# The short convolution's three input projections as seven-multiplication block products

## The chip, the cores and the metric

The kernel runs on one core of one Trainium2 chip. The metric is the device time in microseconds (us) of the whole program, median of three runs. The core has TensorE (PE, matmuls; weight loads are shown as PEld), VectorE (DVE), ScalarE (ACT), GpSimd (POOL) and SyncE (SP, which here only issues DMAs; ScalarE's queue issues some too). All data is float32.

## The reference

A decoder trunk of two layers over 1024 tokens of width 1024. Each layer: a mixer, cross-attention into 256 memory tokens, a squared-ReLU MLP, each behind an RMSNorm and with a residual add. Layer 0's mixer is attention with pooling; layer 1's mixer, which the change is about, is a short gated convolution:

```
def odd_mixer(h, w_in, conv_w, w_out):
    proj = h @ w_in                                  # 1024 -> 3 * 1024
    b_gate = proj[..., :CONV_DIM]
    c_gate = proj[..., CONV_DIM:2 * CONV_DIM]
    z = c_gate * proj[..., 2 * CONV_DIM:]
    zp = jnp.pad(z, ((0, 0), (CONV_WIDTH - 1, 0), (0, 0)))
    y = zp[:, 0:S] * conv_w[0]
    for tap in range(1, CONV_WIDTH):                 # CONV_WIDTH = 3
        y = y + zp[:, tap:tap + S] * conv_w[tap]
    return (b_gate * y) @ w_out
```

## The kernel before, in words

Activations lie transposed: 8 tiles of 128 channels x 1024 tokens. Every float32 matmul operand is cut into a high part `hi` (a rounding copy on ScalarE) and a low part `lo` (what is left, a subtraction on VectorE) by `cut`. A product is then three matmuls, hi*hi, hi*lo and lo*hi, of 128 x 128 weights against 512 tokens.

There are two forms of product. `gemm` makes one tile of 128 output channels: 8 k tiles x 3 x 2 token halves = 48 matmuls (line 201). `split_gemm` makes a pair of output tiles as a 2x2 block product in seven multiplications instead of eight: 7 parts x 4 k pairs x 3 = 84 matmuls (line 277) where two calls of `gemm` have 96. It needs combinations of blocks on both sides. On the weight side `w_cut` makes them from a pair of weight tiles (lines 132 to 160) with four VectorE operations. On the operand's side the class `Split` holds four groups per pair of k tiles: group 0, 1 and 2 of 1024 columns and group 3 of 512, each cut in hi and lo; `combine` (line 257) makes groups 1 to 3 from the scaled raw halves with four VectorE operations. The seven parts accumulate in three PSUM banks, and after each part an `evac` copies or adds a bank to the result (`SPLIT` and `ADDS`; `TAIL` and `TAIL_ADDS` are another order of the same seven, with nine instead of seven additions, in which the first half of both tiles is done after the fifth part). With `first=True` the first four parts run their first three k pairs before the last one, so that the operand's last pair may come late. `hooks` give functions that are called ahead of part i.

The MLP up-projections and down-projections and the cross-attention's queries already use `split_gemm`. The convolution (`conv_mixer`, line 1152) uses `gemm` for its 24 output tiles: for each of 8 channel tiles the gate c, the value x and the gate b; VectorE multiplies each straight out of PSUM, and the norm's factor `rbc` (of the RMSNorm, which is computed beside the first products) is multiplied in there. Its operand is a plain `Act`: 8 pairs of hi and lo. It is made at the end of the first MLP (`mlp`, line 1018, called with the name "m0"): the down-projection m0b runs over four blocks of hidden units c and, for each, four pairs p of output tiles. In each of these 16 products the residual tiles `t` come from DRAM (`look` calls `h_load`) and the parts are added to them; for c < 3 they go back to DRAM (`keep`), and for c = 3 `done` makes the operand of them and adds their squares to the norm (`nn.add`). `A[c]`, the hidden operand, is a `Split` whose groups are fetched from DRAM.

After the projections `residual` (line 828) runs conv_out (named cvo in the profile), one `gemm` per output tile, over `Y`, the 8 tiles of gated results, cut by `Y.put`.

The tile framework's scheduler lays the instructions of each engine in a fixed order at compile time, by readiness and by program order (`tc.high_priority` moves the evacuations ahead). Each engine, SP's and ScalarE's DMA queues too, then works strictly in that order, and waits by semaphores. SBUF has 44 slots of 128 x 1024 (`NSLOT`) for all activations, 4 raw weight tiles (`WR`) and 2 cut ones of each kind; a new weight tile is fetched when a raw one is free (`w_load`, line 113), and cutting runs at most one step ahead of use (`w_next`).

Of the kernel before, what the change touches and what calls it, by code (L numbers as in the profile page):

```python
# [11 lines left out]
F32 = mybir.dt.float32  # L12
# [28 lines left out]
def hybrid_trunk(ctx: ExitStack, tc: tile.TileContext, xT, memT, vecs, lams, rel, onehot, negrow, invcnt,  # L41
# [39 lines left out]
    FLAT = (P, KT, P)  # L81
    order = [(FLAT, w_in[8])]
    for h in range(1, 4):
# [15 lines left out]
    tails = {len(order) - 1}  # L99
    raws, cuts = {}, []  # L100
# [727 lines left out]
    def residual(act, g_col, name, split=False):  # L828
# [3 lines left out]
        r = [None, None]  # L832
        for n in range(KT):
            t = ahead.pop(0)
# [21 lines left out]
            else:  # L856
                ps = gemm(act, f"{name}_{n}")
                nc.vector.tensor_add(t, t, ps)
# [159 lines left out]
    def mlp(l, X, nrm, g_next, name):  # L1018
# [75 lines left out]
        rest = {}  # L1094
        nx, nn = Act(), Norm(f"{name}b")
        fin = g_next is None
        for c in range(4):
            for p in range(KT // 2):
                t, ahead = ahead, []
                tail = fin and c == 3 and p == KT // 2 - 1  # L1100

# [5 lines left out]
                def squares_of(n, h):  # L1107
                    return lambda: nn.add(t[n][:, half(h)], h)
# [4 lines left out]

                todo = [rest, {1: [look]}]
                if p == 0:
# [3 lines left out]
                if c == 0 and p < 2:  # L1119
                    todo.append(late[p])  # L1120
                if tail:
                    todo.append({3: [squares_of(0, 0)], 5: [squares_of(1, 0)], 6: [squares_of(1, 1), lambda: nn.stage1((0,))]})
# [5 lines left out]

                def done(i, t=t, p=p):
                    def run():  # L1130
                        n = 2 * p + i
                        if fin:
                            hd[n] = t[i]
                        else:
                            operand(nx, n, t[i], g_next, f"{name}b")
                        nn.add(t[i])
                    return run

                if c < 3:
                    rest = {2: [keep]}  # L1140
                elif tail:
                    hd.update({2 * p + i: t[i] for i in range(2)})
                    squares_of(0, 1)()
                    rest = {}
                else:
                    rest = {1: [done(0)], 2: [done(1)], 4: [] if fin else [keep]}
        for fns in merged(rest).values():
# [4 lines left out]
    def conv_mixer(X, nrm, g_next, name):  # L1152
        hooks = with_norm(nrm)
        Y = Halves()
        for j in range(KT):
            nm = f"{name}{j}"
            psc = gemm(X, f"{nm}c", hooks.pop(0) if hooks else None)
            cg, z = slot(f"{nm}_cg"), slot(f"{nm}_z")
            if nrm.rbc is not None:
                nc.vector.tensor_mul(cg, psc, nrm.rbc)  # L1160
            psx = gemm(X, f"{nm}x", hooks.pop(0) if hooks else None)
            if j == 0:
                nc.vector.tensor_mul(cg, psc, nrm.rbc)
            nc.vector.tensor_mul(z, psx, nrm.rbc)
            nc.vector.tensor_mul(z, z, cg)
            y = slot(f"{nm}_y")
            nc.scalar.activation(y, z, AF.Copy, scale=col(C_CONV + 16 + j))
            nc.vector.scalar_tensor_tensor(y[:, 1:], z[:, : S - 1], col(C_CONV + 8 + j), y[:, 1:],
                                           op0=ALU.mult, op1=ALU.add)
            nc.vector.scalar_tensor_tensor(y[:, 2:], z[:, : S - 2], col(C_CONV + j), y[:, 2:],  # L1170
                                           op0=ALU.mult, op1=ALU.add)
            nc.vector.tensor_mul(y, y, nrm.rbc)
            psb_ = gemm(X, f"{nm}b")
            nc.vector.tensor_mul(y, y, psb_)
            Y.put(f"{nm}g", j, y)
        return residual(Y, g_next, f"{name}o", split=True)

# [30 lines left out]
def _layout(inp):  # L1208
# [38 lines left out]
    g["pool_w"] = a["pool_w"][0].transpose(1, 0, 2)  # L1247
    g["conv_in"] = tiles(a["conv_w_in"][0])
# [4 lines left out]
    halves = [0, 2, 4, 6, 1, 3, 5, 7]  # L1253
    g["wq"] = tiles(a["xattn_wq"])[..., halves, :]
    g["w1"] = tiles(a["mlp_w1"])[..., halves, :]
# [22 lines left out]
```

## Time and profile before

| | |
|---|---|
| median of three runs | 2549.22 us (2549.22, 2549.35, 2545.19) |
| the profiled execution | 2544.53 us; its span 2542.8 us |
| mean granted TensorE clock | 0.997 |
| PE, PEld, DVE, ACT busy | 98%, 81%, 69%, 42% of the span |
| TensorE instructions | 11522 matmuls (transposes among them) and as many weight loads |
| HBM | 249.91 MB read, 114.03 MB written |

The time holds a launch beside the span of 1.7 us in the profiled execution. A row of the profile's groups reads: line, engine, operation, output <- inputs by the program's names with shapes, count, busy us, mean ns of one, and idle time before it with what ended it. Names: m0a and m0b are the first MLP's up- and down-projection, cv0c, cv0x, cv0b to cv7b the 24 convolution products, cvo conv_out, c1q the next cross-attention's queries; `_x` and `_yz` are PSUM banks, `wr`, `wt`, `wh`, `wl` raw, combined, high and low weights. A matmul's own duration includes its passage through the array, so the distance between starts is what counts.

### The profile page before, as it was taken

The numbers are of one execution on the slowest core, as the hardware profiler recorded it, in microseconds if no ns is written. First come the engines' busy times: TensorE is split into PE (matmuls) and PEld (weight loads), VectorE is DVE, ScalarE is ACT, GpSimd is POOL, SyncE is SP. The second block draws the span as 40 slices with busy tenths as digits, with TensorE's granted clock in tenths as the row PEclk, the third lists the DMA queues.
The fourth block names the chain that finished last, engine by engine and source line by source line (L and its number), as shares of the span: only waits on it lengthen the run. The fifth ranks groups of instructions, "written<-read, shape, count | busy, mean of one in ns | idle before, by whom it ended". The sixth has DMA issues, their size and how long they took to land.

```text
span 2542.8 us, 29713 instructions
## 1 busy us (share of the span) xinstructions
PE 2498.8 (98%) x11522; PEld 2048.1 (81%) x11522; DVE 1763.8 (69%) x2339; ACT 1073.4 (42%) x1513; POOL 25.7 (1%) x24
## 2 busy tenths in 40 slices
PE   9999999999999999999999999999999999999997
PEld 6777778888878888788888888888887888778886
DVE  7777764766677777888784433576667777888876
ACT  5455664445443334443341111344544333434432
POOL 0000000000000000000000000000000000000001
PEclk9999999999999999999999999999999999999998
DMA  5111255221424346877641111422133444777752
GB/s 175 34 34 42 75 169 204 100 83 42 141 88 171 139 145 239 293 270 261 243 154 59 50 50 46 145 75 92 58 117 116 159 160 153 269 266 259 281 207 92
DMA packets 108429, 365.88 MB, mean 144 GB/s; under 512 B 12416, under 2 KB 14848, under 8 KB 108288
## 3 DMA queue, kind: packets, MB, share of 16 engines
q1 hardware_dynamic: 74880, 252.82, 29.5%
q10 hardware_dynamic: 33408, 111.16, 11.4%
q8 instruction: 91, 1.49, 0.2%
q14 instruction: 50, 0.41, 0.0%
HBM read 249.91 MB, written 114.03 MB: 143 GB/s over the span
## 4 chain that ended last, share of the span: by engine, by line
PE 89%; DVE 6%; ACT 2%; DMA 2%; issue 1%; POOL 0%; SPq 0%; ACTq 0%; DVEq 0%; POOLq 0%
PE m0a_x L277 7%; PE m1a_x L277 7%; PE m1b_x L277 7%; PE m0b_x L277 6%; PE m1a_yz L277 5%; PE m0a_yz L277 5%; PE m1b_yz L277 5%; PE m0b_yz L277 4%; PE cvo L201 3%; PE X L201 3%; PE c1o L201 3%; PE c0o L201 3%; PE kv_ps L742 3%; PE qkv L201 2%; PE c1q_x L277 2%; PE c0q_x L277 2%
## 5 line engine op out<-in xcount | busy, mean ns | idle before, releaser
L72 ACT ACTIVATE wh<-wr 128x1024 fp32r<-128x1024 f32 (+1 forms) x318 | 305.6, 961 | 777.7 <-PE m1b_yz L277 137.5
L73 DVE TENSOR_TENSOR wl<-wr,wh 128x1024 fp32r<-128x1024 f32 (+1 forms) x318 | 350.3, 1101 | 135.1 <-ACT wh L72 130.3
L72 ACT ACTIVATE wh<-wt 128x1024 fp32r<-128x1024 f32 x72 | 76.0, 1055 | 60.0 <-PE m0b_x L277 16.5
L73 DVE TENSOR_TENSOR wl<-wt,wh 128x1024 fp32r<-128x1024 f32 x72 | 87.8, 1219 | 0.9 <-ACT wh L72 0.9
L201 PE MATMUL X<-Y,wh 128*128 128x512 f32 x256 | 69.8, 389 | 0.0
L581 ACT ACTIVATE s_p<-s,s_negm 128x128 f32<-128x128 f32 (+7 forms) x64 | 47.3, 739 | 33.6 <-DVE s_negm L580 30.3
L201 PEld LDWEIGHTS X<-Y,wh 128*128 128x128 f32 x256 | 48.1, 188 | 10.0
L149 DVE TENSOR_TENSOR wt<-wr 128x512 f32<-128x512 f32 x71 | 48.8, 687 | 6.8 <-DMA wr<-in_w_dram 3.1
L150 DVE TENSOR_TENSOR wt<-wr,wt 128x512 f32<-128x512 f32 x71 | 48.9, 689 | 1.3
L152 DVE TENSOR_TENSOR wr<-wr,wr 128x512 f32<-128x512 f32 x71 | 48.7, 687 | 1.0
L153 DVE TENSOR_TENSOR wr<-wr,wt 128x512 f32<-128x512 f32 x71 | 48.6, 684 | 0.0
L1028 ACT ACTIVATE m0a_r<-m0a_r 128x1024 f32<-128x1024 f32 x32 | 33.9, 1061 | 32.0 <-DVE m0a_r L1027 31.9
L1028 ACT ACTIVATE m1a_r<-m1a_r 128x1024 f32<-128x1024 f32 x32 | 33.9, 1060 | 32.0 <-DVE m1a_r L1027 31.8
L580 DVE TENSOR_REDUCE s_negm<-s 128x1 f32<-128x128 f32 (+7 forms) x64 | 46.6, 750 | 0.2
L1042 DVE TENSOR_TENSOR m0a_r<-m0a_r,m0a_yz 128x512 f32<-128x512 f32 x32 | 21.9, 685 | 31.3 <-PE m0a_yz L277 31.1
L1042 DVE TENSOR_TENSOR m1a_r<-m1a_r,m1a_yz 128x512 f32<-128x512 f32 x32 | 21.9, 685 | 31.3 <-PE m1a_yz L277 31.1
L1038 ACT ACTIVATE m0a_r<-m0a_x 128x512 f32<-128x512 f32 x32 | 19.1, 598 | 55.7 <-PE m0a_x L277 53.8
L1038 ACT ACTIVATE m1a_r<-m1a_x 128x512 f32<-128x512 f32 x32 | 19.1, 598 | 55.5 <-PE m1a_x L277 53.9
L201 PE MATMUL X<-Y,wl 128*128 128x512 f32 x128 | 40.7, 389 | 0.0
L277 PE MATMUL m0b_x<-m0A,wh 128*128 128x512 f32 x128 | 39.5, 390 | 0.7 <-DVE m0b0h L1112 0.7
L277 PE MATMUL m0a_x<-c0o_x,wh 128*128 128x512 f32 x128 | 39.6, 390 | 0.0
L277 PE MATMUL m1a_x<-c1o_x,wh 128*128 128x512 f32 x128 | 39.5, 390 | 0.0
(2681 smaller groups left out, 7678.9 us busy)
## 6 DMA issues: line engine op xcount, KB each, us to landing
wr<-in_w_dram SPq DMA_DIRECT2D x128, 512.0 KB, 4.0
m0f<-m0a_d SPq DMA_DIRECT2D x48, 512.0 KB, 6.4
m1f<-m1a_d SPq DMA_DIRECT2D x48, 512.0 KB, 6.0
wr<-in_wkv_dram SPq DMA_DIRECT2D x32, 512.0 KB, 3.5
m0a_d<-m0a_r ACTq DMA_DIRECT2D x32, 512.0 KB, 2.8
m1a_d<-m1a_r ACTq DMA_DIRECT2D x32, 512.0 KB, 2.9
wr<-in_conv_in_dram SPq DMA_DIRECT2D x24, 512.0 KB, 3.6
wr<-in_wq_dram SPq DMA_DIRECT2D x16, 512.0 KB, 3.6
```

The lines of the kernel that those rows point to most:

```text
L72: nc.scalar.activation(hi, src, AF.Copy)
L73: nc.vector.tensor_sub(lo, src, f32(hi))
L149: nc.vector.tensor_add(t[:, 4:], b[:, :4], b[:, 4:])
L150: nc.vector.tensor_sub(t[:, :4], a[:, :4], t[:, 4:])
L152: nc.vector.tensor_sub(a[:, :4], b[:, :4], a[:, :4])
L153: nc.vector.tensor_add(a[:, 4:], a[:, 4:], t[:, :4])
L201: nc.tensor.matmul(ps, wt[:, k, :], act.part(k, i, h), start=(k == 0 and wt is hi and i == 0), stop=(k == ks - 1 and wt is lo))
L277: nc.tensor.matmul(banks[b], w[a][:, 4 * (i % 2) + j, :], act.part(g, s, j, c), start=(new and j == 0 and n == 0), stop=(j == nk - 1 and n ...
L580: nc.vector.tensor_reduce(s["negm"][:, m : m + 1], ps[:, :L], axis=AX.X, op=ALU.max, negate=True)
L581: nc.scalar.activation(s["pr"][m][:, :L], ps[:, :L], AF.Exp, bias=s["negm"][:, m : m + 1], accum_out=s["den"][:, m : m + 1])
L742: nc.tensor.matmul(ps[mt], mem["x"][i][k // 4][:, k % 4, mt * P : (mt + 1) * P], w[j][:, kk, :], start=(k == 0 and n == 0), stop=(k == KT ...
L1028: nc.scalar.activation(t, t, AF.Square)
```

## The change

Three edits, which belong together.

1. `conv_mixer` makes its three projections with `split_gemm`: for each of 4 pairs of channel tiles a product for c, x and b, evacuated into two raw tiles each by copies (ScalarE) and additions (VectorE). The gating, the taps, the norm's scaling and the gate b run from these tiles as hooks of the following products; the norm's factor comes in as its square (`squared`) for c*x and once for b. The cutting of the Y tiles 0 to 5 (`parts`) is put into the last pair's products. The weights `conv_in` are fetched in pairs and laid out in halves on the host.
2. Its operand becomes a `Split`, made at the end of m0b. For c = 3, `scale` writes the two tiles' halves, scaled, into raw tiles; `sums` combines them; group 0 is cut at once; the other groups of pairs 0 and 1 go to DRAM (`put`, ScalarE's queue) and come back later (`get`, SP's queue), those of pairs 2 and 3 stay in SBUF; `made` cuts them. Groups 2 and 3, the last norm additions and the norm's two steps lie in the first two convolution products (`nx.late`). The last m0b product now runs in the `TAIL` order, and for c = 3 the next residual tiles are loaded ahead of the sixth part instead of the second.
3. In `residual`, for conv_out alone (`late=True`), the first two output tiles run k = 0 to 5 for both, then k = 6 and 7 for both.

The second MLP, with no norm and operand to prepare, keeps its order. The diff, cut to its core:

```diff
-            for j in range(KT):
-                order += [(FLAT, conv_in[i * KT + j]) for i in (1, 2, 0)]
+            for j in range(KT // 2):
+                order += [(FLAT, conv_in[i * KT + 2 * j], conv_in[i * KT + 2 * j + 1]) for i in (1, 2, 0)]
...
+        if late:
+            two = [(w_next(), psg(f"{name}_0")), (cuts[state["used"]], psg(f"{name}_1"))]
+            state["used"] += 1
+            for ks in (range(KT - 2), range(KT - 2, KT)):
+                for w, ps in two:
+                    for k in ks:
+                        steps([(h, ps[:, half(h)]) for h in range(2)], w, act, k)
...
-                ps = gemm(act, f"{name}_{n}")
+                ps = two.pop(0)[1] if two else gemm(act, f"{name}_{n}")
...
-        nx, nn = Act(), Norm(f"{name}b")
+        nx, nn = Split(f"{name}x"), Norm(f"{name}b")
+        def scale(t, p, h):
+            raws_x[p, 2 * h] = slot(f"{name}x{p}_r{h}")
+            for i in range(2):
+                nc.scalar.activation(raws_x[p, 2 * h][:, i * H : (i + 1) * H], t[i][:, half(h)], AF.Copy,
+                                     scale=col(g_next + 2 * p + i))
+        def sums(p):
+            raws_x[p, 1], raws_x[p, 3] = (slot(f"{name}x{p}_t{i}") for i in range(2))
+            raws_x[p, 3] = raws_x[p, 3][:, :H]
+            combine(raws_x[p, 0], raws_x[p, 2], raws_x[p, 1], raws_x[p, 3])
+        def put(p):
+            for g in range(1, 4):
+                xd[p, g] = dp.tile([P, S if g < 3 else H], F32, name=f"{name}x{p}_d{g}")
+                nc.scalar.dma_start(xd[p, g], raws_x.pop((p, g)))
+        def get(g):
+            for p in range(2):
+                x = slot(f"{name}xf{g}_{p}")
+                raws_x[p, g] = x if g < 3 else x[:, :H]
+                nc.sync.dma_start(raws_x[p, g], xd[p, g])
...
-                tail = fin and c == 3 and p == KT // 2 - 1
+                tail = c == 3 and p == KT // 2 - 1
-                todo = [rest, {1: [look]}]
+                todo = [rest, {5 if c == 3 and not fin else 1: [look]}]
+                if tail and not fin:
+                    todo.append({2: [lambda: get(1)], 4: [lambda: made(1, 0)],
+                                 5: [lambda: scale(t, p, 0), lambda: first_group(p), lambda: made(1, 1)],
+                                 6: [lambda: made(1, 2), lambda: get(2)]})
...
+                elif p < 2:
+                    rest = {1: [lambda t=t, p=p: scale(t, p, 0), lambda t=t, p=p: scale(t, p, 1)],
+                            2: [lambda p=p: first_group(p), lambda p=p: sums(p)], 3: [lambda t=t: nn.add(t[0])],
+                            4: [lambda p=p: put(p), lambda t=t: nn.add(t[1]), keep]}
+                elif p == 2:
+                    rest = {2: [lambda t=t, p=p: scale(t, p, 0), lambda t=t, p=p: scale(t, p, 1)],
+                            3: [lambda p=p: first_group(p), lambda p=p: sums(p)], 4: [keep]}
+                    kept[2] = t
+                else:
+                    scale(t, p, 1)
+                    sums(p)
+                    made(1, 3)
+                    nx.late = ({0: [lambda: get(3)], 1: [lambda: made(2, 0)], 2: [lambda: made(2, 1, 2)],
+                                3: [lambda: made(2, 3)], 4: [lambda: made(3, 0, 1)], 5: [lambda: made(3, 2, 3)],
+                                6: [lambda: nn.add(kept[2][0]), keep]},
+                               {0: [lambda: nn.add(kept[2][1])], 1: [lambda t=t: nn.add(t[0])],
+                                2: [lambda t=t: nn.add(t[1])], 4: [nn.stage1], 5: [nn.stage2]})
...
-        for j in range(KT):
-            psc = gemm(X, f"{nm}c", hooks.pop(0) if hooks else None)
-            psx = gemm(X, f"{nm}x", hooks.pop(0) if hooks else None)
-            nc.vector.tensor_mul(z, psx, nrm.rbc)
-            nc.vector.tensor_mul(z, z, cg)
-            psb_ = gemm(X, f"{nm}b")
-            nc.vector.tensor_mul(y, y, psb_)
-            Y.put(f"{nm}g", j, y)
+        def product(nm, hooks, first=False):
+            r = [slot(f"{nm}_r{n}") for n in range(2)]
+            def evac(n, h, ps, new):
+                d = r[n][:, half(h)]
+                if new:
+                    nc.scalar.activation(d, ps, AF.Copy)
+                else:
+                    nc.vector.tensor_add(d, d, ps)
+            split_gemm(X, nm, evac, hooks, first=first)
+            return r
+        before = X.late[0]
+        for j in range(KT // 2):
+            nm, last = f"{name}{j}", j == KT // 2 - 1
+            c = product(f"{nm}c", merged(before, {4: [parts(0)]} if last else {}), first=(j == 0))
+            x = product(f"{nm}x", X.late[1] if j == 0 else {1: [parts(1)], 3: [parts(2)]} if last else {})
+            hooks = {0: [gate(0)], 1: [taps(0)], 2: [gate(1)], 3: [taps(1)], 4: [scaled(0)], 5: [scaled(1)]}
+            if j == 0:
+                hooks = merged({0: [squared]}, hooks)
+            if last:
+                hooks = merged(hooks, {3: [parts(3)], 5: [parts(4)], 6: [parts(5)]})
+            b = product(f"{nm}b", hooks)
+            before = {1: [times(0)], 2: [times(1)]}
+        for n in range(2):
+            times(n)()
+            parts(KT - 2 + n)()
```

Here `gate(n)` multiplies c by x and by the squared norm factor (two VectorE operations of 1024 columns), `taps(n)` is one scaled copy on ScalarE and two VectorE operations, `scaled(n)` multiplies by the norm's factor and `times(n)` by the gate b (one VectorE operation each).

More of the change, by code (lines that the diff above doesn't have):

```diff
@@ L81, in hybrid_trunk @@
     FLAT = (P, KT, P)
-    order = [(FLAT, w_in[8])]
+    order, tails = [(FLAT, w_in[8])], set()
     for h in range(1, 4):
@@ L826, in operand, with residual @@
         cut(*nx.t[n], t, col(g_col + n))
-    def residual(act, g_col, name, split=False):
+    def residual(act, g_col, name, split=False, late=False):
         nx, nn = (Split(f"{name}_x") if split else Act()), Norm(name)
@@ L1127, in keep, with done, run @@
                         h_store(2 * p + i, t[i], f"{name}b{c}")
[L1129 to L1137, printed above, removed]
                 if c < 3:
                     rest = {2: [keep]}
-                elif tail:
-                    hd.update({2 * p + i: t[i] for i in range(2)})
-                    squares_of(0, 1)()
+                elif fin:
+                    def done(i, t=t, p=p):
+                        def run():
+                            hd[2 * p + i] = t[i]
+                            nn.add(t[i])
+                        return run
+                    rest = {1: [done(0)], 2: [done(1)]}
+                    if tail:
+                        hd.update({2 * p + i: t[i] for i in range(2)})
+                        squares_of(0, 1)()
+                        rest = {}
+                elif p < 2:
[15 more added lines that the diff above has]
+                                2: [lambda t=t: nn.add(t[1])], 4: [nn.stage1], 5: [nn.stage2]})
@@ L1176, in conv_mixer @@
-        return residual(Y, g_next, f"{name}o", split=True)
+        Y, ys = Halves(), {}
+        sq = {}
+        def product(nm, hooks, first=False):
[8 more added lines that the diff above has]
+            return r
@@ new lines, in parts, with squared, gate, run @@
+        def parts(k):
+            return lambda: Y.put(f"{name}g{k}_", k, ys.pop(k))
+        def squared():
+            sq[0] = slot(f"{name}_rsq")
+            nc.scalar.activation(sq[0], nrm.rbc, AF.Square)
+        before = X.late[0]
[3 more added lines that the diff above has]
+            x = product(f"{nm}x", X.late[1] if j == 0 else {1: [parts(1)], 3: [parts(2)]} if last else {})
+            def gate(n, c=c, x=x):
+                def run():
+                    nc.vector.tensor_mul(c[n], c[n], x[n])
+                    nc.vector.tensor_mul(c[n], c[n], sq[0])
+                return run
+            def taps(n, z=c, j=j):
+                def run():
+                    k = 2 * j + n
+                    y = ys[k] = slot(f"{name}_y{k}")
+                    nc.scalar.activation(y, z[n], AF.Copy, scale=col(C_CONV + 16 + k))
+                    for d in (1, 2):
+                        nc.vector.scalar_tensor_tensor(y[:, d:], z[n][:, : S - d], col(C_CONV + 8 * (2 - d) + k),
+                                                       y[:, d:], op0=ALU.mult, op1=ALU.add)
+                return run
+            def scaled(n, j=j):
+                return lambda: nc.vector.tensor_mul(ys[2 * j + n], ys[2 * j + n], nrm.rbc)
+            hooks = {0: [gate(0)], 1: [taps(0)], 2: [gate(1)], 3: [taps(1)], 4: [scaled(0)], 5: [scaled(1)]}
+            if j == 0:
+                hooks = merged({0: [squared]}, hooks)
+            if last:
+                hooks = merged(hooks, {3: [parts(3)], 5: [parts(4)], 6: [parts(5)]})
+            b = product(f"{nm}b", hooks)
+            def times(n, j=j, b=b):
+                return lambda: nc.vector.tensor_mul(ys[2 * j + n], ys[2 * j + n], b[n])
+            before = {1: [times(0)], 2: [times(1)]}
@@ L1178, in hybrid_trunk @@
+        for n in range(2):
+            times(n)()
+            parts(KT - 2 + n)()
+        return residual(Y, g_next, f"{name}o", split=True, late=True)
     X, nrm = cross(0, X, nrm, G_MLP[0], "c0")
@@ L1253, in _layout @@
     halves = [0, 2, 4, 6, 1, 3, 5, 7]
+    g["conv_in"] = tiles(a["conv_w_in"][0])[..., halves, :]
     g["wq"] = tiles(a["xattn_wq"])[..., halves, :]
```

28 lines of the change are left out of this document (9 added, 19 removed).

## Prediction, written before the change was run

> **What bounds the kernel now.** I read the page's busy times, its slices and the head of the chain first.
>
> ```profile
> span 2542.8 us, 29713 instructions
> PE 2498.8 (98%) x11522; PEld 2048.1 (81%) x11522; DVE 1763.8 (69%) x2339; ACT 1073.4 (42%) x1513; POOL 25.7 (1%) x24
> ...
> DVE  7777764766677777888784433576667777888876
> ...
> PE 89%; DVE 6%; ACT 2%; DMA 2%; issue 1%; POOL 0%; SPq 0%; ACTq 0%; DVEq 0%; POOLq 0%
> ```
>
> TensorE is busy 98% of the span and is 89% of the chain. A digit of the slices is 63.6 us; the convolution is the stretch of low VectorE digits in the middle (4 4 3 3). A matmul taken away there shortens the kernel if nothing that feeds TensorE becomes late. The chain from the end of the first MLP (m0b) through the projections (cv) to the output projection (cvo) shows whether anything is late today; columns: start, length, engine, group.
>
> ```profile
> 1330.02 2.72 PE m0b_x L277 x12
> 1332.74 6.80 PE cv0c L201 x30
> 1339.54 0.87 PE m0b_n L332 x8
> ...
> 1356.31 10.88 PE cv0b L201 x48
> ...
> 1584.79 10.88 PE cv7b L201 x48
> 1595.67 64.37 PE cvo L201 x284
> ```
>
> Each piece begins where the one before it ends: TensorE waits for nothing from 1330 to 1660 us, neither at the entry from m0b nor at the exit into cvo. A matmul takes 10.88/48 = 0.2267 us. One seventh of a seven-multiplication product (12 matmuls) takes 2.72 us, also 0.2267 each, so both forms pay the same per matmul. Next, TensorE's waits (total, count, longest), since the kernel already has joints like the new one, and the windows (length; then busy us of PE, PEld, DVE, ACT): eight up-projection products of m0a, a stretch of m0b, its last product, and the middle of the projections.
>
> ```profile
> PE m0a_x L277 <- DVE wl L73: 1.3, 1, 1.3
> PE c0q_x L277 <- ACT c0q_r L920: 1.0, 1, 1.0
> PE m0b_x L277 <- DVE m0b0h L1112: 0.7, 1, 0.7
> PE c1o_b L345 <- POOL c1o_rcol L336: 0.3, 1, 0.3
> ```
>
> ```profile
> 757.00:909.30 152.30, 152.30 (x671) 125.17 (x671) 112.41 (x144) 58.78 (x72) 0.00 (x0) 1.00 0.43 152
> 1254.00:1273.00 19.00, 19.00 (x86) 15.74 (x85) 18.78 (x25) 10.84 (x14) 0.00 (x0) 1.00 0.61 226
> 1313.70:1332.74 19.04, 19.04 (x85) 15.78 (x85) 14.50 (x18) 8.58 (x9) 0.00 (x0) 1.00 0.32 111
> 1367.19:1584.79 217.60, 217.60 (x962) 180.27 (x961) 85.13 (x78) 36.29 (x41) 0.00 (x0) 1.00 0.15 49
> ```
>
> In m0a, whose products are of the kind that the convolution will have, VectorE is busy 112.41/152.30 = 74% and TensorE all the time. Even at 18.78 of 19.00 us (99%) TensorE does not stop. In the projections VectorE has 39%: there is room, and the question is how much of it the change takes, above all at the entry.
>
> **The change, part by part.**
>
> *Fewer matmuls.* Before: 24 products of 48 matmuls, 1152. After: 12 products (a pair of column tiles each) of 7 x 12 = 84, 1008. 144 fewer at 0.2267 us: -32.6 us, all on the path, since the stretch has no gap. The page TensorE: Matmul & The Clock Gate of the Trainium skill (section Back-to-back issue gap) states about 131 ns per 512-column matmul in a sustained stream with weight loads; by that the saving would be an estimated 18.9 us. The trace disagrees (226.7 ns), and the trace decides.
>
> *VectorE in the projections.* The prices of single operations (count, then busy us and mean ns):
>
> ```profile
> L73 DVE TENSOR_TENSOR wl<-wr,wh 128x1024 fp32r<-128x1024 f32 x16 | 19.6, 1222 | 1.2
> L73 DVE TENSOR_TENSOR wl<-wr,wh 128x512 fp32r<-128x512 f32 x8 | 5.5, 691 | 14.6 <-ACT wh L72 14.6
> L149 DVE TENSOR_TENSOR wt<-wr 128x512 f32<-128x512 f32 x8 | 5.5, 685 | 0.0
> L1042 DVE TENSOR_TENSOR m0a_r<-m0a_r,m0a_yz 128x512 f32<-128x512 f32 x16 | 11.0, 685 | 16.3 <-PE m0a_yz L277 16.3
> L1172 DVE TENSOR_TENSOR cv_y<-cv_y,m0b_rbc 128x1024 f32<-128x1024 f32 x8 | 9.8, 1226 | 0.3
> L1168 DVE SCALAR_TENSOR_TENSOR cv_y<-cv_z,vec,cv_y 128x1023 f32<-128x1023 f32 x8 | 10.3, 1284 | 9.8 <-ACT cv_y L1167 9.8
> ```
>
> A pair of weight tiles costs 4 combining operations of 0.685, 3 wide subtractions of 1.22 and a narrow one of 0.69: 7.1 us. A product adds 3 evacuating additions of 0.685 (the other 4 copies go to ScalarE): 2.06. A pair j has three products: 21.3 + 6.2. To it come 4 gating multiplications (4.9), 4 taps of 1.284 (5.1), 2 scalings by the norm (2.45) and 2 multiplications by the gate b (2.44): 42.4 us against 3 x 19.04 = 57.1 us of TensorE, 74%, the share of m0a. The cutting of the Y tiles (two subtractions of 0.685 each) is held back: six tiles fall into the last pair, 8.2 us, so it has 50.6 of 57.1, 89%. The 99% stretch lost nothing, so I charge 0; the ends are 0 and the 0.7 us that m0b's first product waits for an addition.
>
> *The operand at the entry.* Before, m0b's last four products (c = 3) left a plain operand: per tile a scaled copy on ScalarE and one subtraction. After, four groups per pair: per pair four scaled half copies on ScalarE, four combining operations (2.74), three wide subtractions (3.66) and a narrow pair part (0.69): 7.1 us of VectorE instead of two subtractions of 1.28. Adding up for each product of 19.04 us: the second and third of c = 3 have 7.1 (weights) + 7 x 0.685 (additions) + 1.22 + 2.74 + the norm's additions (1.22, then 2.44) = 17.1 and 18.3: room. The last one, in the other order of its seven parts, evacuates with nine additions: 7.1 + 6.2 + group 0 of pairs 2 and 3 (2.44) + combining pair 2 (2.74) + group 1 of pairs 0 to 2 (3.66) = 22.1. It had 14.50 before. The first convolution product has 7.1 + 2.06 + combining pair 3 (2.74) + its group 1 (1.22) + group 2 of four pairs (4.9) + group 3 (2.76) + a norm addition (1.22) = 22.0. Both are over 19.04, by 3.1 and 2.9, together 6.0 us of VectorE work that does not fit beside the matmuls; the next product has only 7.1 + 2.06 + three norm additions and the norm's reductions, about 14, and takes up what can wait. What can wait is the norm addition and part of the weights; the groups cannot. So the loss lies between 0 (as in the 99% stretch) and 6.0; I take half, 3.0, as the overload lasts two products and not one.
>
> After m0b's last matmul the chain is: addition 0.69, two half copies on ScalarE 0.6 each, half the combining 1.4, ScalarE's cut 1.06, subtraction 1.22: 5.6 us before group 1 of pair 3 is there. The first product's order gives it 42 matmuls first, 9.5 us, so it is covered if VectorE is free. The same order in c0q costs 1.0 (an evacuating copy queued behind ScalarE's cuts) and m0a has one wait of 1.3 for weights: I charge 1.0, ends 0 and 2.3. The norm's two steps stand one seventh apart (before, they had more work between them): 0.3, as in c1o, ends 0 and 0.3.
>
> *DRAM and queues.*
>
> ```profile
> m0b3h<-m0b2hd SPq DMA_DIRECT2D x8, 512.0 KB, 6.1
> m0b3hd<-m0b3h ACTq DMA_DIRECT2D x8, 512.0 KB, 2.9
> SPq L113 <- DVE wl L73: 114.6, 18, 14.5
> ```
>
> Pairs 0 and 1 send three tiles each out on ScalarE's queue and take them back on SP's: 2.6 MB each way, 12 issues. The windows of that stretch have a DMA share of 0.32 to 0.61: room. The first fetch is issued in the second seventh of m0b's last product and used in the convolution's second seventh: some 19 us, against 6.1 for a load to land. The loads of the next residual pair move from the second to the sixth seventh: 8.2 us to the first addition and 2.7 more until its bank is needed again, 10.9 against 6.1. Cost 0, ends 0 and the fourth rival's price. ScalarE in the first product: weights 3.8, four copies 2.4, the operand's cuts and copies 9, one square: about 16 of 19.
>
> *conv_out.* Its first two outputs run k = 0 to 5 for both, 72 matmuls, 16.3 us, before tiles 6 and 7 are needed. These need one addition, two multiplications and four narrow subtractions (5.9 us on VectorE) and a 0.6 us copy: covered. Without that order the cover would be some 9 us, still enough. Cost 0, ends 0 and 1.
>
> Sum: -32.6 + 3.0 + 1.0 + 0.3 = -28.3 us.
>
> **The rivals.**
>
> *Nothing is lost:* the list of work is spread so that the entry stays gapless as now. -32.6 to -31: about 2515. For it: the 99% stretch. Against it: every existing joint into a split operand waits at least 1.0.
>
> *The entry becomes one long wait.* If the overload stands ahead of the chain for group 1 in VectorE's order, TensorE waits up to 6.0 + 5.6 + 1.4 (the rest of the combining), 13 us at most, and then starts slowly:
>
> ```profile
> 5.73 1.63 PE L415 MATMUL q0ps<-X0h,w0p0h 128*128 128x512 f32 x2 [5.73 <-ACT X0h L75]
> 8.01 1.05 PE L415 MATMUL q0ps<-X0h,w0p0l 128*128 128x512 f32 x2
> 8.86 1.06 PE L415 MATMUL k0ps<-X0h,w0p0h 128*128 128x512 f32 x2
> 11.04 0.63 PE L415 MATMUL q0ps<-X1h,w0p0h 128*128 128x512 f32 x2
> 11.51 0.62 PE L415 MATMUL q0ps<-X1l,w0p0h 128*128 128x512 f32 x2
> ```
>
> After the 5.73 us wait at the start, two matmuls take 0.85 us, and only later 0.47; at 11.04 five such steps have cost about 2.6 us too much. The same page of the Trainium skill (section What's actually happening) says that TensorE's clock is halved after an idle window of some 3.4 us; by that rule only a wait in one piece pays it, and the trace agrees as far as it shows such a wait. With 13 + 2.6 + 1.3 lost, the gain is 15.7: about 2531. Against it: in c0q the same chain, with the same cuts behind it, waits 1.0.
>
> *VectorE bounds the projections.* In m0a it idles 39.9 us in eight products, 5.0 per product, waiting for parts of them. If none of that could be filled, a product of the last pair would take 16.9 + 5.0 = 21.9 instead of 19.04, 9 us in all, and the other nine 14.1 + 5.0 = 19.1, nothing: with the entry, a gain of 19, about 2528.
>
> *Slower: loads stuck in SP's queue.* A weight load there waits for the raw tile's release, 14.5 us at the longest, and holds what is queued behind it. The three loads of residual pairs in c = 3 have 4.8 us to spare, the three fetches about 9, 5 and 9. If every one stood behind the longest wait: 3 x 9.7 + 5.5 + 9.5 + 5.5 = 50 us lost, 17 more than the gain, about 2564. It decides from an average hold of some 11.5 us. Against it: the same queue carries more loads in the rest of m0b, where TensorE waits 0.7 at the most for a residual tile.
>
> **How the numbers follow.** The profiled execution took 2544.5 us, the other runs 2549.2, 2549.4 and 2545.2; the median stands 4.7 above the profiled one. The sum gives 2516.2 against the profiled time and 2520.9 against the median. I predict 2519, from the mean of the four, 2547.1. Likeliest case 0.60 (its own range 2512 to 2525, from its bounds of 0 and 8.6 lost); nothing lost 0.15; long wait 0.10; VectorE the bound 0.08; stuck loads 0.07, over half of that slower and the rest near nothing. The range reaches from 2544.5 - 32.6 = 2512, less one, to the long wait and 3 us beyond: 2511 to 2534. A change of 0.2% (5 us) is about the least that can be told from none: faster 0.92, same 0.04, slower 0.04.
>
> **What would show it.** TensorE's matmuls fall from 11522 by 144 to 11378 and its busy time by about 33; the projections take 12 pieces of 19.04 us without waits between them; VectorE's low digits there rise to 7 and 8. The waits should name cv0c alone, for groups of the operand or for weights, 1 to 6 us in all, and cvo nothing. HBM writes grow by 2.6 MB. I am wrong if waits for residual tiles appear in c = 3, if products in the middle take more than 19.1 us, or if cv0c waits more than 9 us.

## The result, and the profile after

The changed kernel takes 2527.86 us (median of four runs, 2523.86 to 2531.16) against 2547.20 us for the kernel before (four runs): ratio 0.9924 [0.9903, 0.9945], 19.3 us less. The forecast was 2519 us, 28 us less. The time lies in the forecast range, but a third of the forecast gain is missing.

The profiled execution took 2530.0 us. Its page, the same five parts as before:

```profile
span 2528.1 us, 29708 instructions
PE 2475.9 (98%) x11378; PEld 2023.8 (80%) x11378; DVE 1844.3 (73%) x2465; ACT 1134.4 (45%) x1610; POOL 25.7 (1%) x24
...
DVE  7777765657577778887797777666667777888876
...
HBM read 252.53 MB, written 116.65 MB: 146 GB/s over the span
...
PE 86%; DVE 7%; ACT 3%; DMA 2%; issue 1%; POOL 0%; SPq 0%; DVEq 0%; ACTq 0%; POOLq 0%
```

There are 144 fewer matmuls, 2.62 MB more are written, and the low VectorE digits in the middle (4 4 3 3) have become 7 7 7 7, and the one ahead of them, the end of m0b, has risen from 8 to 9. TensorE's share of the chain has fallen from 89% to 86%. The chain of waits from the end of m0b into the convolution shows where it left TensorE (start, length, engine, group):

```profile
1329.24 2.73 PE m0b_x L277 x12
...
1331.99 0.70 DVE m0b3h L1151
...
1350.54 0.61 DVE cv0c_r L1221
...
1351.19 4.21 PE cv0c_yz L277 x9
...
1577.24 2.72 PE cv3b_x L277 x12
1579.96 0.91 PE cvo L201 x4
```

Before, all of this stretch was TensorE's. Now the chain runs over VectorE and ScalarE from 1332 to 1351 us. From there it is on TensorE again, but for the norm's steps (1379 to 1383 us), to the end of the projections and into cvo. TensorE's waits between 1300 and 1670 us (total, count, longest), and the windows (length; busy us of PE, PEld, DVE, ACT, POOL; granted clock; DMA share; GB/s) of the last product of m0b, the first product of the convolution, six products in the middle, and the last pair:

```profile
PE cv0c_x L277 <- ACT cv0c_r L1219: 3.3, 1, 3.3
PE cv0c_x L277 <- DVE wl L73: 1.6, 1, 1.6
PE cv0c_yz L277 <- DVE cv0c_r L1221: 1.4, 1, 1.4
PE m0b_b L345 <- POOL m0b_rcol L336: 0.7, 1, 0.7
```

```profile
1318.00:1337.23 19.23, 19.23 (x86) 15.90 (x85) 17.09 (x24) 10.78 (x13) 0.00 (x0) 1.00 0.68 249
1337.23:1367.29 30.06, 23.67 (x86) 17.78 (x84) 24.55 (x30) 15.85 (x22) 0.00 (x0) 0.83 0.22 79
1408.37:1522.76 114.39, 114.39 (x505) 94.44 (x505) 79.69 (x91) 40.08 (x53) 0.00 (x0) 1.00 0.18 56
1522.76:1579.96 57.20, 57.20 (x253) 47.22 (x253) 43.29 (x52) 26.21 (x39) 0.00 (x0) 1.00 0.17 55
```

The first convolution product, cv0c, took 30.06 us and not 19.04, with a granted clock of 0.83; the other windows have 1.00. Of these 11.0 us, 6.4 are waits; for the other 4.6 TensorE is busy, but slower (23.67 us for work of 19.04). From the first m0b matmul to the first c1q matmul, that is the whole stretch that the change touches, it is 654.7 us before (1022.4 to 1677.1) and 635.1 after (1026.6 to 1661.7): 19.6 less. Of the 32.6 us of matmuls 13.0 were given back: 0.4 in m0b, 11.0 in cv0c, 1.1 in the first pair's other two products (0.7 of it the norm's wait), 0.2 in the other pairs and 0.3 in cvo. I give this stretch for the experiments too, since the part ahead of it differs between two executions of this kernel by 3.4 us (last section).

What happened within cv0c, first on TensorE (start, duration, tile, wait ahead):

```profile
1339.91 0.50 PE L277 MATMUL cv0c_x<-m0x_0h,wl 128*128 128x512 f32 x1 [1.61 <-DVE wl L73]
...
1348.11 0.80 PE L277 MATMUL cv0c_x<-m0x_0h,wh 128*128 128x512 f32 x1 [3.35 <-ACT cv0c_r L1219]
...
1351.19 0.80 PE L277 MATMUL cv0c_yz<-m0x_0h,wh 128*128 128x512 f32 x1 [1.43 <-DVE cv0c_r L1221]
...
1356.05 0.63 PE L277 MATMUL cv0c_x<-m0x_1h,wl 128*128 128x512 f32 x1
1356.48 0.63 PE L277 MATMUL cv0c_x<-m0x_2h,wh 128*128 128x512 f32 x1
...
1357.44 0.40 PE L277 MATMUL cv0c_x<-m0x_3h,wh 128*128 128x512 f32 x1
```

After the wait of 3.35 us the matmuls start 0.43 us apart, and only at 1357 us they are 0.23 apart again: some 17 matmuls at half speed, about 3.4 us beyond the 6.4 us of waits. The last 1.2 us are steps that are a little longer, most of them at a restart. Then ScalarE, whose copy ended the long wait:

```profile
1344.62 1.06 ACT L72 ACTIVATE wh<-wr 128x1024 fp32r<-128x1024 f32 x1 [4.16 <-PE cv0c_yz L277]
1345.59 1.04 ACT L72 ACTIVATE m0x_3h<-m0x_t 128x1024 fp32r<-128x1024 f32 x1
1346.53 1.04 ACT L72 ACTIVATE m0x_0h<-m0xf 128x1024 fp32r<-128x1024 f32 x1
1347.48 0.58 ACT L1219 ACTIVATE cv0c_r<-cv0c_x 128x512 f32<-128x512 f32 x1
```

ScalarE stood idle for 4.16 us, because the next instruction in its order, a weight cut, needed a buffer that TensorE releases only after the second part. The copy of the first bank, whose last matmul started at 1343.7 us, lay behind this cut and two more. TensorE in turn waited for the copy. On VectorE the addition that ended the third wait lay behind three instructions that nobody was waiting for:

```profile
1347.99 0.68 DVE L149 TENSOR_TENSOR wt<-wr 128x512 f32<-128x512 f32 x1
...
1349.32 1.22 DVE L73 TENSOR_TENSOR m0x_0l<-m0xf,m0x_0h 128x1024 fp32r<-128x1024 f32 x1
1350.45 0.68 DVE L1221 TENSOR_TENSOR cv0c_r<-cv0c_r,cv0c_yz 128x512 f32<-128x512 f32 x1
```

So there are two theories. *Overload*, that of the prediction: VectorE has more to do around the entry than fits beside two products, so less work there shortens the entry. *Order*: the amount does not matter; the copy and the addition that free a bank lie behind instructions that could wait. Beside both, *the clock*: a part of the loss is half speed after a wait.

### The profile page after: what moved, and what is told of

Same layout as the page of the kernel before. It is cut to its first block, busy times and chain, and to the rows that moved or that the text cites. A ratio compares the mean times of both kernels' runs of the same rounds, so it can differ in the third digit from the quotient of the medians.

```text
span 2528.1 us, 29708 instructions
## 1 busy us (share of the span) xinstructions
PE 2475.9 (98%) x11378; PEld 2023.8 (80%) x11378; DVE 1844.3 (73%) x2465; ACT 1134.4 (45%) x1610; POOL 25.7 (1%) x24
## 4 chain that ended last, share of the span: by engine, by line
PE 86%; DVE 7%; ACT 3%; DMA 2%; issue 1%; POOL 0%; SPq 0%; DVEq 0%; ACTq 0%; POOLq 0%
PE m0a_x L277 7%; PE m1a_x L277 7%; PE m1b_x L277 6%; PE m0b_x L277 5%; PE m0a_yz L277 5%; PE m1a_yz L277 5%; PE m1b_yz L277 5%; PE m0b_yz L277 4%; PE cvo L201 3%; PE X L201 3%; PE c0o L201 3%; PE c1o L201 3%; PE kv_ps L742 3%; PE qkv L201 2%; PE c0q_x L277 2%; PE c1q_x L277 2%
## 5 line engine op out<-in xcount | busy, mean ns | idle before, releaser
L72 ACT ACTIVATE wh<-wr 128x1024 fp32r<-128x1024 f32 (+1 forms) x330 | 313.1, 949 | 641.7 <-PE m0b_yz L277 126.1
L73 DVE TENSOR_TENSOR wl<-wr,wh 128x1024 fp32r<-128x1024 f32 (+1 forms) x330 | 358.4, 1086 | 164.5 <-ACT wh L72 157.3
L72 ACT ACTIVATE wh<-wt 128x1024 fp32r<-128x1024 f32 x84 | 88.6, 1055 | 79.4 <-PE m1b_x L277 16.4
L73 DVE TENSOR_TENSOR wl<-wt,wh 128x1024 fp32r<-128x1024 f32 x84 | 102.3, 1218 | 1.4 <-ACT wh L72 1.4
L201 PE MATMUL cvo<-cvg,wh 128*128 128x512 f32 x256 | 69.8, 390 | 0.0
L149 DVE TENSOR_TENSOR wt<-wr 128x512 f32<-128x512 f32 x82 | 56.3, 687 | 6.7 <-DMA wr<-in_w_dram 3.1
L150 DVE TENSOR_TENSOR wt<-wr,wt 128x512 f32<-128x512 f32 x82 | 56.4, 688 | 1.6
L152 DVE TENSOR_TENSOR wr<-wr,wr 128x512 f32<-128x512 f32 x82 | 56.3, 686 | 1.1
L201 PEld LDWEIGHTS cvo<-cvg,wh 128*128 128x128 f32 x256 | 48.0, 188 | 10.4 <-ACT wh L72 0.4
L201 PE MATMUL cvo<-cvg,wl 128*128 128x512 f32 x128 | 40.5, 389 | 0.0
```

The lines of the kernel that those rows point to most:

```text
L72: nc.scalar.activation(hi, src, AF.Copy)
L73: nc.vector.tensor_sub(lo, src, f32(hi))
L149: nc.vector.tensor_add(t[:, 4:], b[:, :4], b[:, 4:])
L150: nc.vector.tensor_sub(t[:, :4], a[:, :4], t[:, 4:])
L152: nc.vector.tensor_sub(a[:, :4], b[:, :4], a[:, :4])
L201: nc.tensor.matmul(ps, wt[:, k, :], act.part(k, i, h), start=(k == 0 and wt is hi and i == 0), stop=(k == ks - 1 and wt is lo))
```

## The experiments

The stretch is the one defined above. Medians stand against those of the kernel before on the same chip.

| kernel | median us | ratio [95%] | stretch us |
|---|---|---|---|
| same_again | 2528.80 | 0.9925 [0.9912, 0.9938] | 634.5 |
| copy_first | 2522.59 | 0.9904 [0.9891, 0.9916] | 629.1 |
| fill_wait | 2522.38 | 0.9908 [0.9895, 0.9921] | 631.4 |
| no_late | 2525.48 | 0.9916 [0.9903, 0.9929] | 634.2 |
| order_all | 2523.69 | 0.9909 [0.9895, 0.9923] | 630.7 |
| pool_sums | 2526.21 | 0.9921 [0.9909, 0.9934] | 634.0 |
| two_groups | 2525.00 | 0.9911 [0.9897, 0.9925] | 629.9 |
| no_tail | 2526.11 | 0.9917 [0.9904, 0.9931] | 634.0 |
| order_tight | 2518.11 | 0.9886 [0.9869, 0.9902] | 625.7 |
| tight_pool | 2521.17 | 0.9893 [0.9878, 0.9907] | 625.7 |

**The changed kernel unaltered**, as the base of the others.

> The changed kernel once more, as the measure for the other kernels beside it. Both theories: about 19 us below the kernel before, the same four waits at the entry (3.3, 1.6, 1.4 and 0.7 us), and the spell of matmuls 0.43 us apart behind the longest.

The four waits are those of the first profile to the tenth (3.3, 1.6, 1.4, 0.7), and the stretch is 0.6 us shorter. So a difference of 0.6 us in the stretch says nothing (two executions are few to tell it by); of the medians, whose runs spread over 8 us, it takes a few us to say something.

**The copy and the addition first.** The weight cut and the operand's groups of the third part are issued behind the first bank's copy and addition:

```diff
+            with ExitStack() as behind:
+                if first and i == 2 and done[0] is not None:
+                    for ins in done:
+                        behind.enter_context(tc.issue_after(ins.ins))
...
-                    nx.late = ({0: [lambda: get(3)], 1: [lambda: made(2, 0)], 2: [lambda: made(2, 1, 2)],
+                    nx.late = ({0: [lambda: get(3)], 2: [lambda: made(2, 0, 1, 2)],
```

> Nothing is left out; only the order in cv0c changes: the first bank's copy on ScalarE ahead of the third weight cut and of group 2's cut, and the addition on VectorE ahead of the subtractions that belong to them. Order theory (the long wait is the copy standing behind three cuts, the first of which waits for a weight buffer that TensorE frees just then): the 3.3 us wait falls to 1 or less, the 1.4 to 0.5 or less, the clock stays full, 2.7 + 0.9 + 3.4 = about 7 us below the changed kernel. Overload theory (VectorE has 3 to 6 us of work too much at the entry): the wait moves to the next thing that VectorE makes, and the time is within 1.5 us of the changed kernel.

TensorE's waits in this stretch, and ScalarE in the same place:

```profile
PE cv0c_x L277 <- DVE wl L73: 1.6, 1, 1.6
PE cv0c_x L277 <- ACT cv0c_r L1225: 1.4, 1, 1.4
PE cv0c_yz L277 <- DVE cv0c_r L1226: 1.1, 1, 1.1
```

```profile
1340.83 1.06 ACT L72 ACTIVATE m0x_3h<-m0x_t 128x1024 fp32r<-128x1024 f32 x1 [4.10 <-DVE m0x_t L260]
1341.79 0.58 ACT L1225 ACTIVATE cv0c_r<-cv0c_x 128x512 f32<-128x512 f32 x1
```

The long wait fell from 3.3 to 1.4 us, no matmul behind it was at half speed, and the stretch is 5.4 us shorter, not the 7 that were expected. The work is the same; only its order changed. The copy still lies behind a cut, now that of the operand's last pair, which waits for VectorE.

**The wait filled.** 14 matmuls into a bank that nobody reads stand ahead of the third part:

```diff
+            if first and i == 2 and name == "cv0c":
+                fill = psb("fill")
+                for n in range(14):
+                    nc.tensor.matmul(fill, ws[1][0][:, 0, :], act.part(0, 0, n % 3, 0), start=True, stop=True)
```

> The changed kernel with 14 matmuls more (3.2 us, their result unused) where TensorE waits 3.3 us; order unchanged. Clock theory (the slow matmuls behind the wait come from the wait's length in one piece): the matmuls behind it stay 0.227 us apart, and the time falls by some 3.4 us although more is computed. Rival (they are slow for what they read or for what else runs then): they stay 0.43 us apart, and the time stays within 0.5 us or grows by up to 3.

TensorE at that place:

```profile
1343.94 0.50 PE L277 MATMUL cv0c_x<-m0x_0h,wh 128*128 128x512 f32 x1 [0.18 <-ACT cv0c_r L1223]
1344.28 0.39 PE L277 MATMUL cv0c_x<-m0x_0l,wh 128*128 128x512 f32 x1
1344.51 0.39 PE L277 MATMUL cv0c_x<-m0x_0h,wl 128*128 128x512 f32 x1
```

The copy comes no sooner, and the other waits are as they were, but the matmuls behind it are 0.23 us apart and not 0.43: the stretch is 3.1 us shorter with more matmuls. The half speed was a cost of its own, and idling was its cause.

**Less for VectorE.** The four combining operations of the third pair go to GpSimd:

```diff
-            combine(raws_x[p, 0], raws_x[p, 2], raws_x[p, 1], raws_x[p, 3])
+            combine(raws_x[p, 0], raws_x[p, 2], raws_x[p, 1], raws_x[p, 3], nc.gpsimd if p == 2 else nc.vector)
```

> The changed kernel, with the four combining operations of pair 2 on GpSimd (1.27 us each by its row of this size) instead of VectorE (0.6 us from start to start). Nothing is left out. Overload theory: VectorE has 2.4 us less in m0b's last product, and TensorE waits 2 us or more less at the entry. Order theory: the 1.6 us wait may shrink, the 3.3 us wait and the slow spell stay, as ScalarE's cut waits for TensorE's buffer and not for VectorE; within 1.5 us of the changed kernel.

```profile
PE cv0c_x L279 <- ACT cv0c_r L1221: 3.3, 1, 3.3
PE cv0c_yz L279 <- DVE cv0c_r L1223: 2.1, 1, 2.1
```

Four operations of 0.68 us are gone from VectorE ahead of the entry, and the waits for weights and for the copy are the same. The one for the addition is 2.1 us, as it is in no_late too. The stretch is 634.0 against 634.5 us. Overload expected 2 us less of waits or more. But VectorE waits right ahead of the entry anyway, as its last operand cut of m0b shows, in the changed kernel and in this one:

```profile
1334.57 1.23 DVE L73 TENSOR_TENSOR m0x_3l<-m0x_r,m0x_3h 128x1024 fp32r<-128x1024 f32 x1 [1.29 <-ACT m0x_3h L72]
```

```profile
1329.85 1.23 DVE L73 TENSOR_TENSOR m0x_3l<-m0x_r,m0x_3h 128x1024 fp32r<-128x1024 f32 x1 [1.29 <-ACT m0x_3h L72]
```

In both it is idle for 1.29 us, until ScalarE has made the high part, and starts this operation 2.66 us ahead of cv0c's first matmul. So the four operations lie in front of an idle time, and what this run shows is that m0b's last product hands no overload on. It takes nothing from VectorE within cv0c. GpSimd took 1.9 to 2.3 us for each, not the 1.27 expected, and two VectorE operations that ran meanwhile took 1.20 and 1.71 us where the same ones take 0.69 and 1.22 in same_again.

**Fewer groups.** Groups 2 and 3 of the operand are neither sent to DRAM nor fetched nor cut; group 0 stands in their place:

```diff
-            for g in range(1, 4):
+            for g in range(1, 2):
...
-            for p in range(2):
+            for p in range(2) if g == 1 else ():
...
+                    nx.g[g, p] = nx.g[0, p]
```

> The changed kernel with groups 2 and 3 of the convolution's operand left out: group 0 stands in for them, so four wide and four narrow cuts on ScalarE and as many subtractions on VectorE are missing from the first product, and two thirds of the DRAM traffic. Order theory: one cut less stands ahead of the copy, so the 3.3 us wait falls to about 2.3, the 1.4 one to 0.5, and the 1.6 one stays; 2 to 4 us below the changed kernel. Overload theory: with 7 us of VectorE work gone all waits but the first vanish; 8 us below or more.

```profile
PE cv0c_x L277 <- ACT cv0c_r L1223: 2.4, 1, 2.4
```

The cut of m0x_0 ahead of the copy is gone, and the wait is one cut (0.95 us) shorter; the other two cuts and their 4.55 us of idle ScalarE are still there. The addition's wait is gone too, with the subtraction that lay right ahead of it; the wait for weights is 1.6 us as before. The stretch is 4.6 us shorter. The total alone would fit both theories, since by the prediction's prices some 7.7 us of VectorE's work are gone; that the copy's wait shrinks by just its one cut speaks for the order. The addition's wait fits both. Behind the 2.40 us the matmuls were at half speed too, for 3.4 us:

```profile
1347.24 0.63 PE L277 MATMUL cv0c_x<-m0x_0l,wh 128*128 128x512 f32 x1
1347.66 0.63 PE L277 MATMUL cv0c_x<-m0x_0h,wl 128*128 128x512 f32 x1
```

**Without the late order of conv_out** (the third edit):

```diff
-        return residual(Y, g_next, f"{name}o", split=True, late=True)
+        return residual(Y, g_next, f"{name}o", split=True)
```

> The changed kernel without its third edit: conv_out's first two outputs one after the other. My step (42 matmuls, some 9.5 us, cover the 6 us that tiles 6 and 7 take after the last product): no wait at cvo, within 1 us of the changed kernel. Rival (the edit is needed, as VectorE has other work in hand there): waits of 2 to 6 us at cvo, and as much slower.

No wait at cvo in this kernel either, and 634.2 against 634.5 us in the stretch: the third edit does nothing here.

**The last m0b product in its old order** of parts, so that group 0 of the last pair is made only after its last part:

```diff
-        tails.add(len(order) - 1)
+    tails.add(len(order) - 1)
...
-                split_gemm(A[c], f"{name}b{c}_{p}", evac, merged(*todo), tail=tail)
+                split_gemm(A[c], f"{name}b{c}_{p}", evac, merged(*todo), tail=tail and fin)
```

> The changed kernel with m0b's last product in the usual order of its seven parts, so that group 0 of pair 3 can only be made after the last part. My step (the other order takes group 0 off the end): the chain addition, copies, cut, subtraction takes some 4.5 us and group 1's 4 us more, against 4.1 and 9.5 us of matmuls that need neither, so TensorE waits 1 to 4 us more. Rival (the two additions more that the other order costs weigh as much): within 1 us of the changed kernel.

The waits shift among themselves (4.1 for the copy, 1.0 for the addition, 0.4 for the operand's last pair, the wait for weights gone), and the stretch is 634.0 us. The 1 to 4 us more of waits that were expected did not come. So this order of parts, too, is worth nothing that shows while the copy is late; with the copy in time it was not tried.

**More of the order.** Beside copy_first, group 1 of pair 1 and group 1 of the last pair are cut later, and the norm's second step moves by one part:

```diff
-                                 5: [lambda: scale(t, p, 0), lambda: first_group(p), lambda: made(1, 1)],
-                                 6: [lambda: made(1, 2), lambda: get(2)]})
+                                 5: [lambda: scale(t, p, 0), lambda: first_group(p)],
+                                 6: [lambda: made(1, 1), lambda: made(1, 2), lambda: get(2)]})
...
-                    made(1, 3)
-                    nx.late = ({0: [lambda: get(3)], 2: [lambda: made(2, 0, 1, 2)],
+                    nx.late = ({0: [lambda: get(3)], 2: [lambda: made(1, 3), lambda: made(2, 0, 1, 2)],
...
-                                2: [lambda t=t: nn.add(t[1])], 4: [nn.stage1], 5: [nn.stage2]})
+                                2: [lambda t=t: nn.add(t[1])], 4: [nn.stage1], 6: [nn.stage2]})
```

> Nothing is left out. As copy_first, and besides: group 1 of pair 3 is cut behind the first bank's copy and addition (in copy_first the copy stood behind that cut, which waited for VectorE's combining), group 1 of pair 1 is cut behind the first product's first weights (the 1.6 us wait), and the norm's second step moves one seventh later (the 0.7 us wait). Order theory: the waits at the entry fall from 4.8 us in copy_first to 2 or less, some 3 us below copy_first and 8 below the changed kernel. Overload theory: VectorE has no free microsecond there, so what is moved back is waited for instead; within 1 us of copy_first.

This missed. The waits for weights, for the copy and for the norm are gone, but one of 4.4 us came in their place. Its row, and VectorE at that place:

```profile
PE cv0c_yz L277 <- DVE cv0c_r L1225: 4.4, 1, 4.4
```

```profile
1338.48 0.69 DVE L149 TENSOR_TENSOR wt<-wr 128x512 f32<-128x512 f32 x1
...
1342.41 0.68 DVE L1225 TENSOR_TENSOR cv0c_r<-cv0c_r,cv0c_yz 128x512 f32<-128x512 f32 x1
```

The bank for the addition was full at about 1338.3 us; six operations went ahead of it, none of which TensorE needed yet. Behind this wait the matmuls were at half speed for 6 us. The stretch is 630.7 us, worse than copy_first with its three short waits.

**The order, tight.** The combining of the last pair and all that follows is put behind the addition, and later parts' work behind the subtraction of the last pair's group 1:

```diff
-                if first and i == 2 and done[0] is not None:
-                    for ins in done:
+                if first and i >= 2 and done[0] is not None:
+                    for ins in done[:2]:
                         behind.enter_context(tc.issue_after(ins.ins))
+                    if i > 2:
+                        behind.enter_context(tc.issue_after(act.gate.ins))
...
-                    sums(p)
-                    nx.late = ({0: [lambda: get(3)], 2: [lambda: made(1, 3), lambda: made(2, 0, 1, 2)],
+                    nx.late = ({0: [lambda: get(3)], 2: [lambda: (sums(3), made(1, 3), made(2, 0, 1, 2))],
```

> Nothing is left out. As order_all, but combining pair 3 and cutting its group 1 come behind the first product's copy and first addition on VectorE too, and the next products' weights behind that cut; in order_all the addition stood behind the next product's two weight combinations and pair 3's four, and its 4.4 us were waited for in one piece. Order theory: the amount of VectorE work is the same, yet no wait above 1 us is left at the entry, at most 2 us in all, and the clock stays full: the stretch from m0b to c1q is 9 to 11 us shorter than in the changed kernel, the time 2517 to 2520. Overload theory: VectorE's queue is full, so the wait only moves to group 1 of pair 3: 3 to 5 us of waits again, and the time of order_all.

TensorE's waits, the addition on VectorE with the operation behind it, and the window of cv0c:

```profile
PE cv0c_x L279 <- DVE m0x_2l L73: 0.7, 1, 0.7
PE cv0c_x L279 <- DVE m0x_3l L73: 0.5, 1, 0.5
PE cv0c_x L279 <- ACT cv0c_r L1227: 0.2, 1, 0.2
```

```profile
1338.89 0.68 DVE L1228 TENSOR_TENSOR cv0c_r<-cv0c_r,cv0c_yz 128x512 f32<-128x512 f32 x1
1339.49 0.68 DVE L261 TENSOR_TENSOR m0x_t<-m0x_r,m0x_r 128x512 f32<-128x512 f32 x1
```

```profile
1332.87:1355.03 22.16, 20.72 (x86) 15.22 (x84) 22.06 (x28) 16.15 (x21) 0.00 (x0) 1.00 0.30 104
```

VectorE works as much as before, back to back, but the addition now goes ahead of the combining. 1.4 us of waits are left and none starts a spell of half speed: 625.7 us, 29.0 below the kernel before, and 2518.11 us in all, the lowest median of those run. The stretch is 8.8 us shorter than in same_again, a little under the 9 to 11 expected. With the same work cv0c takes 22.16 us, not 30.06: this is what shows the order to be the cause of most of the loss. The 3.1 us that are left over 19.04 stand beside a VectorE that is busy for 22.06 of the 22.16 us, and two of the three waits are for its subtractions.

**The tight order with less for VectorE** (order_tight with the edit of pool_sums):

> order_tight with the four combining operations of pair 2 on GpSimd instead of VectorE. Nothing is left out. Order theory: once the order is right VectorE's amount of work at the entry no longer counts, and the time is that of order_tight within 1 us. Overload theory: 2.4 us less on VectorE shorten the entry by 1 to 2.4 us more.

The same three waits, and 625.7 us in both. With the order right, too, the work in m0b's last product is worth nothing; here too VectorE idles 1.29 us behind it, ahead of the entry. The median is 3 us above order_tight's, though the profiled execution (2516.72 us) is not; where the other runs lost them no profile shows. So no overload comes over from m0b. Whether less work for VectorE within cv0c would take off any of its last 3.1 us no run tests without also changing what stands ahead of the copy.

## Why the prediction was right and where it was wrong

- *Fewer matmuls, -32.6:* right. 144 fewer, and order_tight shows that 29.0 of it can be had. TensorE's busy time fell by 22.9 us (2498.8 to 2475.9) and not by about 33, as matmuls at half speed are busy for longer: 4.6 us in cv0c, and some 4 us more are lost ahead of m0b, where nothing was changed (last section).
- *VectorE in the projections, 0:* right. Behind cv0c no product waits for an evacuation, and the nine of the last three pairs take 19.07 us each; VectorE's share is 79.69/114.39 = 70% (forecast 74%), in the last pair 43.29/57.20 = 76% (89%).
- *DRAM and queues, 0:* right. No wait names a residual tile or a fetched group, and writes grew by 2.62 MB (2.6).
- *conv_out, 0:* right; without the late order it is 0 too.
- *The norm's steps, 0.3:* 0.7, over the end of 0.3 that was named.
- *The operand at the entry, 4.0:* wrong, the term that was mis-sized. cv0c lost 11.0 us: 1.6 of waiting for weights, 3.3 for the copy, 1.4 for the addition, 3.4 of half speed and 1.2 of longer steps, where the text put 3.0 for VectorE's overload and 1.0 for the copy. The overload explains little of it. Half of it was to come from m0b's last product, which had 17.09 us of VectorE's work in 19.23 (22.1 forecast) and an idle VectorE behind it. In cv0c VectorE is indeed full, but order_tight does the same work with 7.9 us less; at most the 3.1 us left there can be its price. That they are close to the 3.0 forecast is no proof of that term, which was half of an overload in two products. For the copy it took the 1.0 us of c0q as the price, because the same cuts lie there; it did not ask what the first of these cuts waits for. Here it waits for a buffer that TensorE holds up to the second part's last matmul, so that the copy can only come three cuts later. No term of the sum stood for an order that holds up a bank.
- *The 1 to 6 us of waits at cv0c:* 6.4, just outside of what was named, and mostly for the copy and the addition, not for groups or weights; "more than 9 us", which was to prove it wrong, is exceeded if the half speed is counted.
- *The time:* 2527.86 us lies outside the 2512 to 2525 of the likeliest case. It lies in the whole range because that was stretched to hold the long wait.

Of the rivals, *one long wait* had the place and the price of the slow start about right (2.6 us named, 3.4 measured), and its 2531 us is nearer to 2527.9 than the forecast's 2519. Its mechanism is not quite what happened: TensorE waited for a bank and not for group 1, 3.35 us in one piece and not up to 13. *VectorE bounds the projections* gave 2528, the very number, for a wrong reason, as the products in the middle show. *Nothing is lost* did not come true even in the best version, which lost 3.7 us of the 32.6. Loads stuck in SP's queue left no wait.

The prediction took it that only a wait in one piece, of some 3.4 us, is paid with a slow start. That is borne out in part: 1.4 us in copy_first left matmuls 0.23 us apart, and 3.35 us here, 4.1 in no_tail and 4.4 in order_all left them 0.43 apart. But the 2.40 us of two_groups did so too, and in no_late and pool_sums the three matmuls behind the 3.35 us ran at full speed, and only those behind the next wait, of 2.1 us, at half. The first two of the three, in no_late:

```profile
1343.86 0.50 PE L277 MATMUL cv0c_x<-m0x_0h,wh 128*128 128x512 f32 x1 [3.35 <-ACT cv0c_r L1219]
1344.19 0.39 PE L277 MATMUL cv0c_x<-m0x_0l,wh 128*128 128x512 f32 x1
```

So the length of one wait does not decide it alone. The Trainium skill, TensorE: Matmul & The Clock Gate, section What's actually happening, puts the idle window at about 3.4 us and lets it run freely. The 2.40 us wait does not agree with a limit of 3.4 us; a window that runs freely would fit the same 3.35 us being followed by half speed in one run and not in another, but no run here tests that.

## What to carry to other kernels

Beside an engine's load, read its order: find the copy or addition that frees a PSUM bank, look at what lies ahead of it in its engine's order, and ask what each of those waits for. A cut that needs a buffer which TensorE still holds stalls everything behind it, and TensorE in the end; issuing such work behind the copy gained 5 us here, and the whole order some 9 us. Where TensorE must wait anyway, look at the distance of the matmuls behind the wait: filling it with matmuls that nobody reads kept the clock here and gained 3.1 us. In copy_first the waits are short, 1.6 us at most, and no half speed followed them either.

## What the runs showed of the hardware beyond that

A spell of half speed outlasts its cause: after 3.35 us of waiting matmuls were 0.43 us apart for 8.8 us (with a further 1.43 us wait in it), after 4.4 us for 6 us, after 2.40 us for 3.4 us. And it comes without a long wait too. In the attention part, which no edit here touches, the profiles of after, two_groups and no_tail have such a spell at about 300 us (granted clock 0.88 to 0.92 from 300 to 340 us), and those of the kernel before and of the other eight do not (1.00). The window in the profile of after:

```profile
300.00:340.00 40.00, 40.00 (x186) 30.82 (x186) 21.88 (x32) 22.24 (x37) 0.00 (x0) 0.89 0.35 107
```

and the same in the unaltered second run:

```profile
300.00:340.00 40.00, 39.90 (x201) 30.54 (x202) 25.14 (x38) 26.72 (x45) 0.00 (x0) 1.00 0.40 124
```

In the 40 us ahead of it TensorE is equally busy in both (38.29 us, the rest in three waits of 0.9 us or less), yet the granted clock behind is 0.89 in one and 1.00 in the other, and 15 matmuls fewer start. All that follows comes 3.4 us later (m0b begins at 1026.6 and at 1023.2 us), where the runs of this kernel differ by 8 us in all. What decides it was not tried.

VectorE's operations overlap at their ends: of those of 0.68 and 1.22 us the next one starts 0.60 and 1.13 us later. A sum of durations overstates a full VectorE by some 8 to 13%, which is part of why the overload was put too high.
